# Gated delta branch: the log-decay sums as rows from two products, spread over the partitions through DRAM, and a pinned copy

## Chip, cores and metric

The kernel runs on one core of a Trainium2 chip. The metric is the device time of one execution in microseconds (us), lower is better. Five engines work side by side, each through its own instruction stream in order: TensorE (PE, with PEld for its weight loads), VectorE (DVE), ScalarE (ACT), GpSimd (POOL) and SyncE (SP), which here issues all transfers.

## What is computed

Two models of two layers each run one after the other on 256 tokens of width 1024: first feed-forward blocks, a hybrid mixer and a sparse attention, then a second model whose layers have three branches (a gated MLP, a retention, a gated delta rule) that are gated, projected and summed. The change touches only the gated delta branch, once in each of the two layers of the second model. Cut to what matters, for one direction:

```python
gc = jnp.cumsum(to_chunks(g[..., None], c)[..., 0], axis=-1)
decay = jnp.exp(jnp.where(incl, gc[..., :, None] - gc[..., None, :], -jnp.inf))
lower = jnp.where(strict, jnp.einsum("nbhid,nbhjd->nbhij", kb, kc) * decay, 0.0)
sol = lax.linalg.triangular_solve(lower + eye, rhs, left_side=True, lower=True)
```

`g` is the log decay of every token and head. The decay matrix needs its running sums once along the rows and once along the columns. There are 4 heads and two directions, forward and backward.

## The kernel before

**Staging.** Weights stream through SBUF in units of 1 MB (`raw`, three buffers, line 258). Each unit is turned in two halves into a high part (ACT, line 203) and a low part (DVE, line 207), with four buffers of halves, and each matrix product is three matmuls (lines 277 to 279). SP issues a load when the DVE part of the unit three before is done.

**Order.** A scheduler places the instructions of each engine by priority, which is program order, and by simulated times; an instruction that is ready earlier may float ahead. `keep_in_program_order` pins an instruction behind the instruction that was traced last on its engine.

**Two strands.** In `second` (line 191) a generator `delta` (line 206, the gated delta branch) is woven with a generator `others` (line 1491, gates, projections and the other branches). Each `yield n` in `delta` lets `others` trace n steps. The numbers stand in `SIDE` (line 1158). Steps 2 and 3 of `others` are a product of two weight units, 4 and 5 the next product, 6 and 7 the first half of a gate (`half(0, 0)`), 8 a small product of the MLP branch with the first unit of `half(0, 1)`.

**The stage of the change.** In `delta`, in order:

1. `narrow` and `softplus` give the log decays `gs` (lines 1212 to 1226), a tile of 128 tokens by 16 columns (direction, token half, head).
2. `keys(0, ...)` (line 1259) makes the keys `k` from two weight units. After each, one step of `others` is traced (2 and 3).
3. `yield SIDE[0]` traces steps 4 and 5 of `others`.
4. Four products (lines 1263 to 1266) give the running sums as columns, and line 1268 copies them to `gc`.
5. For each of four pairs of direction and token half, four products (line 1275) give the sum of one head each, repeated on all partitions: the column of `gs`, broadcast to 128 x 128, times a triangular mask. From that PSUM tile, DVE subtracts the column and caps into `D` (line 1279), ACT takes an Exp for the other chunk into `Dc` (line 1282, two of four pairs), and ACT an Exp over `D` (line 1283).
6. `scores` (line 1292) multiplies keys with keys (line 1297, PE) and with `D` and `Dc` (lines 1301 and 1305, DVE) into `U`.
7. POOL adds the two directions (line 1312), `yield SIDE[1]` traces steps 6 and 7, and `U[0]` goes to DRAM (line 1331) and comes back in blocks of 32 (line 1335). ACT turns one half of them (line 1337), and POOL solves the blocks in 31 steps (lines 1341 and 1343). ACT turns one half back (line 1344), SP sends the result to DRAM (lines 1350 and 1352) and fetches it again (line 1353) as `C`.
8. `yield SIDE[2]` traces step 8. Then come the queries (`keys(1, ...)`), their scores, the values (lines 1365 to 1370) and the copies of `C` (lines 1384 and 1386, ACT) that the rest of the solution is built on.

Of the kernel before, what the change touches and what calls it, by code (L numbers as in the profile page):

```python
# [12 lines left out]
AF = mybir.ActivationFunctionType  # L13
OP = mybir.AluOpType
AX = mybir.AxisListType
PSUM = bass.MemoryType.PSUM

D = 1024
T = 256
# [27 lines left out]
class Entry:  # L47
# [17 lines left out]
    def load(self, dram, between=None):  # L65
        self.raw.append(self.net.fetch(dram, 2048, between))
# [38 lines left out]
class Net:  # L105
# [43 lines left out]
    def dram(self, shape):  # L149
        self.n += 1  # L150
        return self.dp.tile(shape, F32, name=f"dram{self.n}")

    def load_const(self, name, cols, parts=128):
        t = self.const(cols, parts=parts)
# [348 lines left out]
    def start(self, dram):  # L503

        nc = self.nc
        self.x = [self.cp.tile([128, D], F32, name=f"x{t}") for t in range(2)]
        halves = lambda n: [slice(o, o + n // 2) for o in (0, n // 2)]
# [6 lines left out]
        with self.manual(mybir.EngineType.SP):  # L514
            a, b = halves(D)
            load(0, a)
# [337 lines left out]
def _parts(x, n, bits):  # L854

    out = []
    for _ in range(n):
# [9 lines left out]
         "Y00 C10 U11 C11 Q01 Y01 C12 | C13 M110 | M111 X10 |  | Y10 X11 |  | Q10 Q11 Y11 |  |  |  |  |  | "  # L867
         "W0 | D | W1 | D | ")
SHARE = ((0, 0), (0, 0), (1, 1), (1, 1), (1, 1), (1, 1))
# [285 lines left out]
            pass  # L1155


SIDE = (2, 2, 1, 1, 1, 1, 1, 1, 1, 2, 0)


class Second:
# [29 lines left out]
    def second(self, l, then, end=None):  # L1191
        nc, ins = self.nc, self.ins
        V, A, PE, G = nc.vector, nc.scalar, nc.tensor, nc.gpsimd
        mm = PE.matmul
# [4 lines left out]
        v4 = lambda a: a.rearrange("p (h c) -> p h c", h=4)  # L1199
# [6 lines left out]
        def delta(y_c):  # L1206

            yield SIDE[7]
            Y = [v24(self.g(1024)) for _ in range(2)]
# [14 lines left out]
            gs = self.small(16)  # L1224
# [13 lines left out]
            def keys(i, ss):  # L1238
# [3 lines left out]
                for gr in range(2):  # L1242
# [10 lines left out]
                    out.append(a)  # L1253
                    yield SIDE[8 + i]
                V.tensor_scalar(ss, pss[:, :8], EPS, None, op0=OP.add)
                return [out[h // 2][:, h % 2] for h in range(4)]

            ss, r, rq, nk = self.small(16), None, self.small(8), self.small(8)
            k = yield from keys(0, ss[:, :8])
            yield SIDE[0]  # L1260

            pc = self.pt()
            mm(pc[:, 0:8], self.tri, gs[:, 0:8], start=True, stop=True)
            mm(pc[:, 8:16], self.rtri, gs[:, 8:16], start=True, stop=True)
# [2 lines left out]
            gc = self.small(24)  # L1267
            V.tensor_copy(gc, pc[:, :24])
            D = [v24(self.g(1024)) for _ in range(2)]
            Dc = [v4(self.l2()) for _ in range(2)]  # L1270
            for d, t in order:
                pr = v4(self.pt())
                for h in range(4):
                    c = d * 8 + t * 4 + h
                    mm(pr[:, h, :], gs[:, c:c + 1].to_broadcast([128, 128]), self.rtri if d else self.tri,  # L1275
                       start=True, stop=True)
                for h in range(4):
                    c = d * 8 + t * 4 + h
                    V.scalar_tensor_tensor(D[d][:, t, h, :], pr[:, h, :], gc[:, c:c + 1], self.rcap if d else self.cap,
                                           op0=OP.subtract, op1=OP.min)  # L1280
                    if t != d:
                        A.activation(Dc[d][:, h, :], pr[:, h, :], AF.Exp, bias=gc[:, 16 + d * 4 + h:17 + d * 4 + h])
                A.activation(D[d][:, t], D[d][:, t], AF.Exp)

            rk = self.small(8)
# [26 lines left out]
            G.tensor_tensor(U[0], U[0], U[1], OP.add)  # L1312
            yield SIDE[1]

# [11 lines left out]
            B, turn = sq(flat(U[1])), sq(flat(X))  # L1326
            Z, back = sq(flat(Y[0])[:, :512]), flat(Y[0])[:, 512:].rearrange("p (i q) -> p i q", q=16)
            lower = slice(64, 128)
# [4 lines left out]
            for d in (1, 0):  # L1333
                for s in range(2):
                    nc.sync.dma_start((turn if d else B)[parts[d][s]],
                                      bass.AP(wide.tensor, wide.offset, [[129 * 32, 32], [128, 32], [1, 32]]))
            A.activation(B[lower].rearrange("p j i -> p i j"), turn[lower], AF.Copy)
            for e in range(31):
                n, m, cs = 31 - e, e // 2 + 1, slice(e + 1, 32)
                a = flat(Y[1])[:, :m * n].rearrange("p (q i) -> p q i", i=n)  # L1340
# [5 lines left out]
            for d in range(2):  # L1346
# [6 lines left out]
                nc.sync.dma_start(C[d].rearrange("p (m c) -> p m c", m=8), tight.rearrange("(m r) j c -> (r j) m c", r=4))  # L1353
            yield SIDE[2]
            q = yield from keys(1, ss[:, 8:])
            r = self.rsqrt(ss, 16, 1.0, 0.0)
# [7 lines left out]
            for gr in range(2):  # L1364
                ps = self.group_w(ww[4 + gr], hT)
                for j in range(2):
                    acc = conv(8 + 2 * gr + j, ps[j][:, :256])
                    for t in range(2):
                        c = (2 * gr + j) * 128
                        PE.transpose(pv[t][:, c:c + 128], acc[:, t * 128:(t + 1) * 128], self.ident)  # L1370
                yield SIDE[10]
            for t in range(2):
# [18 lines left out]
            for t in range(2):  # L1391
                for d in range(2):
                    c = C[2 * d].rearrange("p (t h c) -> p t h c", t=2, h=4)[:, t, :, None].to_broadcast([128, 4, 4, 32])
                    (G if d else V).tensor_tensor(r4(Y[d][:, t]), r4(bc4(self.near)), c, OP.mult)
            for lev in range(2):
                flip()
                T1 = []
                for t in range(2):
                    p = v4(self.pt())
# [5 lines left out]
                for t in range(2):  # L1405
                    p = v4(self.pt())
                    for h in range(4):
                        mm(p[:, h, :], T1[t][:, h, :], Y[1][:, t, h, :], start=True, stop=True)
                    a, b, keep = Y[0][:, t], Y[1][:, t], T1[t]
# [8 lines left out]
            for i in range(3):  # L1418
                for d in range(2):
                    a, b = (1, 0) if d else (0, 1)  # L1420
                    p = v4(self.pt())
                    for h in range(4):
                        if i == 1:
                            mm(p[:, h, :], Uc[d][:, h, :], W[d][:, a, h, :], start=True, stop=True)
                        else:
                            mm(p[:, h, :], Y[d][:, b if i else a, h, :], (r1[d] if i else vp[a])[:, h, :],
                               start=True, stop=True)
# [6 lines left out]
            for t in range(2):  # L1434
                po = v4(self.pt())
                d = 1 - t
# [13 lines left out]
                for h in range(4):  # L1450
                    V.scalar_tensor_tensor(v4(yo)[:, h, :], po[:, h, :], f[:, h:h + 1], v4(zd[t])[:, h, :],
                                           op0=OP.mult, op1=OP.mult)
# [161 lines left out]
        out = self.down_steps(ins["bout"][l], 8, mT.tok, self.add_x if then else self.finish(end), then)  # L1614
# [195 lines left out]
```

## Time and profile before

| | |
|---|---|
| median of 3 runs | 1719.06 us (1717.37 to 1719.6) |
| profiled execution, its own time | 1717.73 us |
| span of the profiled execution, first to last instruction | 1715.9 us |
| mean granted TensorE clock | 0.992 |
| busy PE / DVE / ACT / POOL | 98% / 66% / 52% / 17% of the span |
| DMA | 287.65 MB, mean 168 GB/s |
| longest chain, by engine | PE 82%, DVE 6%, POOL 5%, issue 3%, ACT 2%, DMA 2% |
| the two layers of the second model | from about 1095 to 1400 us and from 1400 us to the end |

The busy share of PE is an average and counts pipelined matmuls. What tells more is where PE sat idle, and which instruction it then waited for. Times below are positions in the span, in us from its first instruction; the second layer repeats the stage of the change some 308 us later.

### The profile page before, as it was taken

The page shows a single profiled execution, that of the slowest core. Times are in us where ns is not written, and L with a number is a line of the kernel's source. Part 1 is how long each engine was busy: PE and PEld are TensorE (multiplying, and loading weights), DVE is VectorE, ACT ScalarE, POOL GpSimd, SP SyncE. Part 2 cuts the span into 40 slices and gives each one's busy share as a digit, 9 for nine tenths or more (in the row PEclk, how much of TensorE's full clock was granted, in tenths as well). Part 3 has the DMA queues.
Part 4 walks back from the last instruction along what each step waited for, and adds up shares of the span by engine and source line. Part 5 has one row for each costly group of instructions (what it writes and reads, how often), then busy time and mean ns, then how long its engine had stood idle before and what let it go on. Part 6 is the DMA issues. An engine that isn't in the chain of part 4 may idle for free.

```text
span 1715.9 us, 27060 instructions
## 1 busy us (share of the span) xinstructions
PE 1686.2 (98%) x10518; PEld 1495.0 (87%) x10518; DVE 1130.9 (66%) x2203; ACT 896.4 (52%) x1329; POOL 299.4 (17%) x458
## 2 busy tenths in 40 slices
PE   9999999999999999999899999999999999999998
PEld 8998799788999899988689998888898878889886
DVE  7665588656665566647956664657775765778566
ACT  7443476464444354434465444567446446644643
POOL 3000021002000010000331000234532113364211
PEclk9999999999999999999899999999999999999999
DMA  7555453444555555554125556445443544554442
GB/s 274 197 176 205 150 193 127 147 152 159 194 193 188 176 193 191 182 205 161 68 99 180 189 189 212 167 153 168 142 151 143 184 165 175 149 163 158 146 148 96
DMA packets 63440, 287.65 MB, mean 168 GB/s; under 512 B 23760, under 2 KB 26704, under 8 KB 30288
## 3 DMA queue, kind: packets, MB, share of 16 engines
q1 hardware_dynamic: 63312, 285.92, 48.3%
q8 instruction: 83, 1.36, 0.3%
q14 instruction: 45, 0.37, 0.1%
HBM read 283.28 MB, written 2.62 MB: 167 GB/s over the span
## 4 chain that ended last, share of the span: by engine, by line
PE 82%; DVE 6%; POOL 5%; issue 3%; ACT 2%; DMA 2%; SPq 0%; POOLq 0%; ACTq 0%; DVEq 0%
PE mm L278 25%; PE mm L279 25%; PE mm L277 24%; DVE lo L207 2%; POOL g L1343 2%; POOL g L1341 2%; DMA g<-dram 1%; PE tr L435 1%; ACT hi L203 1%; DVE g L85 0%; DVE g L1010 0%; PE tr L1275 0%; PE tr L1583 0%; PE tr L687 0%; PE tr L1401 0%
## 5 line engine op out<-in xcount | busy, mean ns | idle before, releaser
L207 DVE TENSOR_TENSOR lo<-raw,hi 128x512 fp32r<-128x512 f32 (+1 forms) x1032 | 696.5, 718 | 433.4 <-ACT hi L203 432.2
L203 ACT ACTIVATE hi<-raw 128x1024 fp32r<-128x1024 f32 (+1 forms) x526 | 546.7, 1045 | 542.9 <-PE mm L279 239.6
L278 PE MATMUL mm<-g,hi 128*128 128x256 f32 x1760 | 496.7, 282 | 0.0
L277 PE MATMUL mm<-g,hi 128*128 128x256 f32 x1760 | 495.3, 282 | 0.8 <-ACT hi L203 0.8
L279 PE MATMUL mm<-g,lo 128*128 128x256 f32 x1760 | 495.8, 283 | 0.0
L277 PEld LDWEIGHTS mm<-g,hi 128*128 128x128 f32 x1760 | 333.2, 189 | 2.2 <-ACT hi L203 1.2
L278 PEld LDWEIGHTS mm<-g,hi 128*128 128x128 f32 x1760 | 333.1, 189 | 0.7
L279 PEld LDWEIGHTS mm<-g,lo 128*128 128x128 f32 x1760 | 332.4, 189 | 0.3 <-issue 0.2
L277 PE MATMUL mm<-hi,g 128*128 128x512 f32 (+1 forms) x784 | 313.2, 400 | 0.7 <-ACT g L203 0.7
L278 PE MATMUL mm<-lo,g 128*128 128x512 f32 (+1 forms) x784 | 311.5, 398 | 1.2 <-DVE lo L207 0.7
L279 PE MATMUL mm<-hi,g 128*128 128x512 f32 (+1 forms) x784 | 309.6, 396 | 1.0 <-DVE g L448 1.0
L279 PEld LDWEIGHTS mm<-hi,g 128*128 128x128 f32 x784 | 147.7, 189 | 35.9 <-DVE g L448 1.9
L278 PEld LDWEIGHTS mm<-lo,g 128*128 128x128 f32 x784 | 148.1, 189 | 35.1 <-DVE lo L207 5.0
L277 PEld LDWEIGHTS mm<-hi,g 128*128 128x128 f32 x784 | 148.0, 189 | 32.5 <-ACT g L203 1.2
L278 PE MATMUL mm<-lo,f 128*128 128x512 f32 x416 | 164.7, 396 | 0.2 <-POOL lo L207 0.2
L279 PE MATMUL mm<-hi,f 128*128 128x512 f32 x416 | 163.9, 396 | 0.0
L277 PE MATMUL mm<-hi,f 128*128 128x512 f32 x416 | 161.4, 398 | 0.0
L214 POOL TENSOR_SCALAR sm<-sm 128x1 f32<-128x1 f32 x18 | 7.8, 431 | 576.7 <-ACT c L70 576.0
L278 PEld LDWEIGHTS mm<-lo,f 128*128 128x128 f32 x416 | 78.1, 188 | 19.5 <-POOL lo L207 0.6
L279 PEld LDWEIGHTS mm<-hi,f 128*128 128x128 f32 x416 | 78.1, 188 | 18.6
L277 PEld LDWEIGHTS mm<-hi,f 128*128 128x128 f32 x416 | 78.1, 188 | 18.2
L90 POOL TENSOR_TENSOR g<-x,g 128x512 f32<-128x512 f32 x12 | 15.4, 1292 | 216.1 <-DVE x L499 170.2
(408 smaller groups left out, 1666.8 us busy)
## 6 DMA issues: line engine op xcount, KB each, us to landing
raw<-in_wgw_dram SPq DMA_DIRECT2D x80, 1024.0 KB, 4.9
raw<-in_wdn_dram SPq DMA_DIRECT2D x44, 1024.0 KB, 4.9
raw<-in_bx_dram SPq DMA_DIRECT2D x24, 1024.0 KB, 4.8
raw<-in_bgate_dram SPq DMA_DIRECT2D x24, 1024.0 KB, 4.8
raw<-in_bw_dram SPq DMA_DIRECT2D x20, 1024.0 KB, 4.8
raw<-in_hyx_dram SPq DMA_DIRECT2D x12, 1024.0 KB, 4.8
raw<-in_bproj_dram SPq DMA_DIRECT2D x12, 1024.0 KB, 4.9
raw<-in_hyw_dram SPq DMA_DIRECT2D x10, 1024.0 KB, 4.9
```

The lines of the kernel that those rows point to most:

```text
L90: self.nc.gpsimd.tensor_tensor(self.src[t][:, s], self.net.x[t][:, s], self.gain[:, s], OP.mult)
L203: nc.scalar.activation(hi, src, AF.Copy)
L207: (nc.gpsimd if o and help else nc.vector).tensor_tensor(lo[..., s], src[..., s], hi[..., s].bitcast(F32), OP.subtract)
L214: G.tensor_scalar(r, v, add, EPS, op0=OP.add, op1=OP.add)
L277: mm(out, a[0], b[0], start=start, stop=False)
L278: mm(out, a[0], b[1], start=False, stop=False)
L279: mm(out, a[1], b[0], start=False, stop=stop)
L435: self.nc.tensor.transpose(p[:, k, :], src[:, k * 128:(k + 1) * 128], self.ident)
L1341: G.tensor_tensor(a, Z[:, :m, e:e + 1].to_broadcast([128, m, n]), B[:, e:e + 1, cs].to_broadcast([128, m, n]), OP.mult)
L1343: G.tensor_tensor(Z[:, :m, cs], Z[:, :m, cs], a, OP.add)
```

## The change

The running sums of the 8 columns of one direction are made as 8 rows by one product (columns of `gs` as the stationary side, the triangular mask as the moving side), two products in all. ACT copies the two 8 x 128 results to SBUF, one transfer writes them to DRAM (8 KB), and two transfers read them back (8 rows of 128 for each direction), the same 4 KB to every partition, straight into `D` (512 KB each). The products are pinned behind the keys. `yield SIDE[0]` (steps 4 and 5) moves behind the two reads. The subtraction works in place in `D`, so the Exp for the other chunk is now traced ahead of it. Two instructions of that loop are pinned, the first subtraction and the first Exp for the other chunk of each such pair. Step 8 of `others` is traced ahead of the turning copy (line 1337) instead of behind the solution, and that copy is pinned.

```diff
+    def rows(self, products):
+        nc, n, b = self.nc, products[0][0].shape[-1], len(products)
+        p, r = self.pt(), self.t2()
+        for i, (cols, mask) in enumerate(products):
+            self.tc.keep_in_program_order(nc.tensor.matmul(p[:n, i * 128:(i + 1) * 128], cols, mask, start=True, stop=True))
+        nc.scalar.activation(r[:n, :b * 128], p[:n, :b * 128], AF.Copy)
+        d = self.dram([b, n, 128])
+        nc.sync.dma_start(d.rearrange("b n c -> n b c"), r[:n, :b * 128].rearrange("n (b c) -> n b c", b=b))
+        return d
+
+    def spread(self, out, d, first, n):
+        self.nc.sync.dma_start(out, bass.AP(d.tensor, d.offset + first * 128, [[0, 128], [1, n * 128]]))
...
-SIDE = (2, 2, 1, 1, 1, 1, 1, 1, 1, 2, 0)
+SIDE = (2, 2, 0, 1, 1, 1, 1, 1, 1, 2, 0)
...
             k = yield from keys(0, ss[:, :8])
-            yield SIDE[0]
-
+            gs_rows = self.rows([(gs[:, 0:8], self.tri), (gs[:, 8:16], self.rtri)])
             pc = self.pt()
...
             D = [v24(self.g(1024)) for _ in range(2)]
+            for d in range(2):
+                self.spread(D[d].rearrange("p t h c -> p (t h c)"), gs_rows, 8 * d, 8)
             Dc = [v4(self.l2()) for _ in range(2)]
+            yield SIDE[0]
             for d, t in order:
-                pr = v4(self.pt())
                 for h in range(4):
                     c = d * 8 + t * 4 + h
-                    mm(pr[:, h, :], gs[:, c:c + 1].to_broadcast([128, 128]), self.rtri if d else self.tri,
-                       start=True, stop=True)
-                for h in range(4):
-                    c = d * 8 + t * 4 + h
-                    V.scalar_tensor_tensor(D[d][:, t, h, :], pr[:, h, :], gc[:, c:c + 1], self.rcap if d else self.cap,
-                                           op0=OP.subtract, op1=OP.min)
                     if t != d:
-                        A.activation(Dc[d][:, h, :], pr[:, h, :], AF.Exp, bias=gc[:, 16 + d * 4 + h:17 + d * 4 + h])
+                        i = A.activation(Dc[d][:, h, :], D[d][:, t, h, :], AF.Exp, bias=gc[:, 16 + d * 4 + h:17 + d * 4 + h])
+                        if h == 0:
+                            self.tc.keep_in_program_order(i)
+                    i = V.scalar_tensor_tensor(D[d][:, t, h, :], D[d][:, t, h, :], gc[:, c:c + 1],
+                                               self.rcap if d else self.cap, op0=OP.subtract, op1=OP.min)
+                    if c == 0:
+                        self.tc.keep_in_program_order(i)
                 A.activation(D[d][:, t], D[d][:, t], AF.Exp)
...
-            A.activation(B[lower].rearrange("p j i -> p i j"), turn[lower], AF.Copy)
+            yield 1
+            self.tc.keep_in_program_order(A.activation(B[lower].rearrange("p j i -> p i j"), turn[lower], AF.Copy))
```

## Rows read from the trace of the kernel before

**Rows 1.** The page's first part: busy us, share of the span, instructions.

```profile
PE 1686.2 (98%) x10518; PEld 1495.0 (87%) x10518; DVE 1130.9 (66%) x2203; ACT 896.4 (52%) x1329; POOL 299.4 (17%) x458
```

**Rows 2.** Windows of 10 us: width, busy us (instructions) of PE, PEld, DVE, ACT, POOL, clock, DMA.

```profile
1150.00:1160.00 10.00, 10.00 (x61) 8.90 (x61) 7.84 (x25) 7.08 (x14) 3.40 (x4) 1.00 0.34 124
...
1220.00:1230.00 10.00, 7.62 (x40) 6.03 (x40) 5.38 (x11) 3.98 (x6) 0.00 (x0) 1.00 0.78 234
```

**Rows 3.** Waits of PE, 1070 us to the end: total us, times, longest.

```profile
PE tr L1370 <- DVE t L1235: 4.4, 4, 1.4
```

**Rows 4.** Timeline of ACT, first layer: start, us, instruction, idle before and its releaser.

```profile
1215.95 1.10 ACT L1344 ACTIVATE g<-g 64x512 f32<-64x512 f32 x1 [9.02 <-POOL g L1343]
...
1225.42 0.42 ACT L1386 ACTIVATE g<-g 128x256 f32<-128x256 f32 x1 [5.61 <-DMA g<-dram]
```

**Rows 5.** Timeline of SP: issues of weight loads on both sides of the transfers of the solution.

```profile
1203.39 0.33 SPq L258 DMA_DIRECT2D raw<-in_bx_dram  x1
...
1218.76 0.61 SPq L258 DMA_DIRECT2D raw<-in_bw_dram  x1
```

**Rows 6.** Timeline of POOL: the addition, the first and the last step of the solution.

```profile
1168.67 2.39 POOL L1312 TENSOR_TENSOR g<-g,g 128x1024 f32<-128x1024 f32 x1 [15.18 <-DVE g L1301]
...
1182.12 0.24 POOL L1341 TENSOR_TENSOR g<-g,g 128x31 f32<-128x31 f32 x1 [11.06 <-ACT g L1337]
...
1215.68 0.23 POOL L1343 TENSOR_TENSOR g<-g,g 128x16 f32<-128x16 f32 x1
```

**Rows 7.** Timeline of PE: the products of the sums (a product is two instructions).

```profile
1136.98 0.28 PE L1263 MATMUL tr<-sm,c 128*128 128x8 f32 x2
...
1149.81 3.82 PE L1275 MATMUL tr<-c,sm 128*128 128x128 f32 x32
1153.38 0.48 PE L277 MATMUL mm<-hi,g 128*128 128x512 f32 x1
```

**Rows 8.** DVE: a window over the decay stage (columns of Rows 2), then its timeline.

```profile
1150.98:1168.78 17.80, 17.80 (x95) 15.26 (x94) 15.78 (x48) 12.03 (x22) 2.53 (x4) 1.00 0.34 119
...
1139.81 1.29 DVE L207 TENSOR_TENSOR lo<-raw,hi 128x512 fp32r<-128x512 f32 x2 [3.02 <-ACT hi L203]
...
1150.98 1.12 DVE L1279 SCALAR_TENSOR_TENSOR g<-tr,sm,c 128x128 f32<-128x128 f32 x4 [0.70 <-PE tr L1275]
...
1168.44 0.34 DVE L1305 SCALAR_TENSOR_TENSOR l<-l,sm,tr 128x128 f32<-128x128 f32 x1
```

**Rows 9.** Groups by line and shape: total us, mean ns | idle before, releaser.

```profile
L196 ACT ACTIVATE t<-tr 16x256 f32<-16x256 f32 x2 | 0.7, 352 | 0.0
...
L1282 ACT ACTIVATE l<-tr,sm 128x128 f32<-128x128 f32 x16 | 5.2, 361 | 3.0 <-DVE g L1279 3.0
...
L1279 DVE SCALAR_TENSOR_TENSOR g<-tr,sm,c 128x128 f32<-128x128 f32 x32 | 9.3, 342 | 2.6 <-PE tr L1275 1.4 <-ACT l L1282 1.2
...
L85 DVE SCALAR_TENSOR_TENSOR g<-x,sm,g 128x512 f32<-128x512 f32 x8 | 5.6, 748 | 3.8 <-POOL sm L217 3.8
```

**Rows 10.** DMA issues by tensor: count, KB each, median us from issue to landing.

```profile
raw<-in_bgate_dram SPq DMA_DIRECT2D x24, 1024.0 KB, 4.8
...
g<-dram SPq DMA_DIRECT2D x12, 128.0 KB, 4.9
...
f<-in_gln_dram SPq DMA_DIRECT2D x2, 512.0 KB, 3.7
...
dram<-g SPq DMA_DIRECT2D x8, 64.0 KB, 2.4
```

**Rows 11.** Timeline of SP and ACT where the new transfers and the copies would stand.

```profile
1137.74 1.09 ACT L1511 ACTIVATE f<-mm 128x512 f32<-128x512 f32 x2
...
1141.16 0.33 SPq L258 DMA_DIRECT2D raw<-in_bgate_dram  x1
...
1161.03 1.06 ACT L203 ACTIVATE hi<-raw 128x1024 fp32r<-128x1024 f32 x1
...
1179.92 2.12 ACT L1337 ACTIVATE g<-g 64x1024 f32<-64x1024 f32 x1 [0.48 <-DMA g<-dram]
```

## The prediction, made before the changed kernel ran

> **What bounds the kernel now.** I read the page first. PE is busy in 98% of the span and no other engine is near that [rows 1], so an edit pays if it takes work from PE or closes one of its few gaps. Busy shares by window come next. Where the sums are made PE has no gap (10.00 of 10 us), but behind the block solution it has one (7.62 of 10 us) [rows 2]. The waits name it: the transposes of line 1370 waited 4.4 us in four waits, 2.2 us a layer [rows 3].
>
> That gap is the end of a chain, read backwards. ACT stood 9.02 us until POOL had finished its 31 steps, then 5.61 us until the solution was back from DRAM at 1225.42 [rows 4]. SP issues in order too: between its weight loads of 1203.39 and 1218.76 stand the writes that wait for POOL [rows 5]. So ACT and SP stand still, the stock of converted weights runs out, and PE stops. POOL starts its 31 steps at 1182.12, after the addition of 1168.67 and the way through DRAM, and ends them at 1215.91 [rows 6]. The addition waits for the last score on DVE, at 1168.44 to 1168.78, and the DVE stage that ends there starts at 1150.98 [rows 8]. **At this one place the start of the decay stage sets the end, and not PE's work alone.** Elsewhere it is PE's work.
>
> **Part 1, PE.** Removed: 16 products a layer, 32 instructions, from 1149.81 to the start of the next at 1153.38, 3.57 us or 0.112 us each [rows 7]. Added: two products, which move the same 128 columns, four instructions, 0.45 us (bounds: 0.28 us for two instructions with few columns, so 0.56 us, and nothing) [rows 7]. Net 3.1 us a layer. They lie on PE's own path.
>
> **Part 2, when the decays start.** The two row products are pinned behind the keys' last traced step, where the first product of the column sums already stood, at 1136.98 [rows 7]. The steps to the landing:
> - ACT's copy of 8 x 256 is near the copy of 16 x 256, 0.35 us [rows 9]. It stands behind the two copies that end at 1138.83 [rows 11], so it is done at about 1139.2.
> - The write of 8 KB I price as the 64 KB writes, 2.4 us (below 2.4 it may be; above, the 512 KB load, 3.7) [rows 10]: 1141.6. SP's issue waits for it. A weight load of 1141.16 [rows 11] may be caught behind the wait for under 1 us; its second half is converted at 1161.03 [rows 11], and a load lands in 4.8 us [rows 10], so some 14 us hide it.
> - The two reads of 512 KB have no like: no transfer in this trace reads one row for all partitions. The nearest are 3.7 us for 512 KB alone and 4.9 for the small reads from DRAM, some of which queue behind a weight load [rows 10]. With that load in front I take 5.5 for the first, which lands at 1147.1, and 1.1 more for the second (4.8 less 3.7, the price of 512 KB more [rows 10]), at 1148.2. Below: 3.7 from 1141.6, at 1145.3. Above: each read takes a whole load's 4.8 and both stand behind one load, 1151.2 and 1156.0.
>
> DVE is no bar: the first subtraction is pinned behind the last conversion of step 5, and counting conversions back from PE's order that is the pair at 1139.81 [rows 8]. So the stage starts at 1147.1 instead of 1150.98, 3.9 us earlier.
>
> **Part 3, the length of the stage.** It lasts 17.80 us, 15.78 of them busy on DVE [rows 8]. A subtraction costs 342 ns from PSUM. From SBUF it is worth the same: 748 ns for 512 columns [rows 9] leaves 342 at 128, if each column costs 1.06 ns. An Exp costs 361 ns [rows 9] at most from either. That the Exp now goes ahead of the subtraction in place is no new kind of wait: today the two waited for each other as well, 3.0 and 1.2 us over both layers [rows 9]. The scores need not wait for PSUM tiles that the sums held. Of the 2.02 us in which DVE stood I take half away, 1.0 (bounds: nothing, and 2.0). Together the chain to the addition ends 4.9 us earlier.
>
> **Part 4, step 8 and the turning copy.** The same steps of the other strand are traced in total, so no work is added. The pin puts the copy behind step 8's second conversion, which ran at 1161.03, long before the copy at 1179.92 [rows 11]; 4.9 us earlier it is still behind. Nothing, with 14 us of cover; if that cover were gone, 1.06 us for one conversion [rows 11].
>
> **Sum.** At the gap PE arrives 3.1 us earlier, and the solution 4.9. PE's gap of 2.2 shrinks to 0.4, so the layer ends 4.9 us earlier; the most is 3.1 + 2.2 = 5.3. Two layers: 9.8 us, at most 10.6. The profiled execution took 1717.73 us by itself, 1.3 under the median; its span of 1715.9 would be 1706.1. I put the sum on the median: 1719.06 - 9.8 = **1709.3 us**.
>
> **A rule that would change the sum.** No row shows the rate of 128 partitions that read the same 4 KB; a plain load of 1 MB takes 4.8 us [rows 10]. The Trainium skill, in DMA: Bandwidth & Descriptors, section Latency and other measured facts, reports that rows which fall on the same HBM channels are read at about half rate (207 against 103 GB/s), and calls the mechanism an inference. No run here shows it yet.
>
> **Rivals.**
> 1. *The reads at half rate.* Each 512 KB costs 1.1 us more [rows 10], so the second lands 2.2 us later and the chain is 2.7 us earlier. Two layers give 5.4: 1713.7. For it: all rows are one address. Against: 4 KB reads are as long as those of a load. The rule above is this case.
> 2. *PE's saving alone.* The gap of line 1370 is gone or stays for its own reasons, because the engines' orders are made anew. Gain 2 x 3.1 = 6.2: 1712.9. For it: PE waited there for DVE, not by name for the solution [rows 3]. Against: the two waits of ACT just ahead [rows 4].
> 3. *The change does not do what it says.* The copy, the write or the conversions are placed so that the decays start no earlier. Then PE arrives 3.1 us earlier at a solution that comes when it did, and the gap grows from 2.2 to 5.3. Gain nothing: 1719. For it: the wait for POOL and the one for DRAM bind ACT today [rows 4], so less PE work alone is worth nothing there. Against: gaps on ACT and DVE around 1139 to 1150 leave room [rows 8, 11].
> 4. *Slower: the reads land late.* DVE stands at the pinned subtraction while the conversions of the next weights queue behind it. With 1.0 from part 3 the gain is gone when the stage starts at 1152.0, and 0.2% is lost from 1153.7. By the upper bound of part 2 the second read lands at 1156.0; the second of the four pairs needs it, about 1.1 us into the stage (four subtractions, 1.12 [rows 8]), so that the stage counts as starting at 1154.9. Then 2.9 us a layer are lost, 5.8 in all: 1724.9. For it: two transfers and a wait in a row in place of a product that needed none, in a queue that also carries the weights. Against: every row of a like size lands in under 5 us [rows 10].
>
> **How the numbers follow.** A measurement of this kernel tells about 0.2%, 3.4 us, from no change. The forecast has 0.50, rival 1 0.10, rival 2 0.07, rival 3 0.18, rival 4 0.15. Faster: 0.50 + 0.10 + 0.07 = 0.67; same 0.18; slower 0.15. The forecast's own range is 1706.5 (the most, 10.6, less the 2 us by which runs differ) to 1713. The range reaches up through rivals 1 to 3 and over the milder part of rival 4, to 1721, and leaves out the rest of it, about one in ten, and some of the low end.
>
> **What would show it.** No products at line 1275 and two new ones at about 1137. The first subtraction before 1149, the addition on POOL near 1164, the first of the 31 steps near 1177, the last near 1211. ACT's wait at line 1386 no longer than today's, and the waits of line 1370 near 0.8 in total. Part 2 is wrong if the reads land more than 10 us after the write; part 3, if the window from the first subtraction to the last score is over 18 us; the chain as such, if POOL starts earlier and PE still ends where it did. The whole prediction is wrong if PE has a new gap of several us between 1137 and 1180.

## The result, and the profile after

The changed kernel is slower by 0.6%: median 1729.37 us (20 runs, 1726.73 to 1736.79) against 1718.20 us for the kernel before on the same chips (20 runs, 1715.74 to 1740.3). The ratio is 1.0059, 95% interval 1.004 to 1.0078. The forecast was 1709.3 us, with 1721 as the upper end. The profiled execution after took 1729.21 us, span 1727.4, 11.5 more than the span before.

Line numbers after are 15 to 18 higher. The page's first part first:

```profile
PE 1685.4 (98%) x10462; PEld 1491.0 (86%) x10462; DVE 1129.3 (65%) x2203; ACT 898.1 (52%) x1333; POOL 302.9 (18%) x458
```

There are 56 matmul instructions fewer than in [rows 1], 28 a layer as predicted, and yet the span is longer. The timeline of PE in the first layer (start, us, instruction, idle time before it and its releaser) shows the parts of the change in place, and where the time went:

```profile
1135.77 0.60 PE L158 MATMUL tr<-c,sm 128*8 128x128 f32 x4
...
1148.62 0.39 PE L292 MATMUL mm<-hi,g 128*128 128x512 f32 x1
1148.84 0.39 PE L293 MATMUL mm<-lo,g 128*128 128x512 f32 x1
...
1226.06 0.66 PE L1388 MATMUL tr<-c,t 128*128 128x128 f32 x2 [5.94 <-DVE t L1250]
...
1227.80 0.63 PE L292 MATMUL mm<-hi,g 128*128 128x512 f32 x1
1228.23 0.63 PE L293 MATMUL mm<-lo,g 128*128 128x512 f32 x1
```

The four instructions of the row products stand at 1135.77. At 1226.06 PE comes out of a gap of 5.94 us, before the same transposes that waited 2.2 us a layer in [rows 3]. Behind it a product of 512 columns follows the last one after 0.43 us; at 1148 it was 0.22. The waits of PE from 1070 us to the end (total us, times, longest) hold both layers:

```profile
PE tr L1388 <- DVE t L1250: 11.5, 2, 5.9
PE mm L292 <- DVE t L1250: 4.1, 4, 1.4
```

The first row was 4.4 before; the second is new. Windows of 10 us (the columns of [rows 2]; the last three numbers are granted clock, DMA share, GB/s):

```profile
1150.00:1160.00 10.00, 10.00 (x46) 8.30 (x45) 8.06 (x23) 8.78 (x15) 2.55 (x2) 1.00 0.51 183
1180.00:1190.00 10.00, 7.47 (x50) 6.29 (x49) 5.96 (x10) 9.15 (x14) 8.08 (x19) 1.00 0.48 175
...
1220.00:1230.00 10.00, 4.06 (x13) 3.19 (x12) 7.72 (x15) 5.65 (x9) 0.00 (x0) 0.76 0.73 228
1230.00:1240.00 10.00, 10.00 (x44) 8.05 (x43) 3.70 (x7) 4.27 (x5) 2.04 (x2) 0.90 0.41 136
...
1540.00:1550.00 10.00, 9.67 (x34) 7.77 (x35) 6.02 (x12) 2.39 (x4) 0.00 (x0) 0.70 0.60 211
```

In 1220 to 1230 PE is busy for 4.06 us (7.62 in [rows 2]) and the clock is 0.76: part of the window ran at 1.2 instead of 2.4 GHz, which is what the doubled spacing of the products shows. In the second layer the same comes at 1540.

**The balance.** The idle gaps of PE in the second model (from 1070 us on) sum to 22.2 us after and 10.2 before, so +12.0: the transposes 11.5 against 4.4, and 4.9 in new gaps around 1184 to 1188 and in layer two. The clock missing in the windows under full clock (10 us times one minus the clock, without the last window) is 10.2 us after and 5.1 before, so about +5.1. Behind the two long gaps alone it is 6.8; a stretch of low clock at 1120 to 1140, ahead of the change, was 1.7 us shorter in this execution. The removed products give back about 5.8 (measured below). 12.0 + 5.1 - 5.8 = 11.3, of 11.5. The clock term is rough; in the experiments the same balance is off by 1 to 3 us.

**Why PE starves at 1220.** The timeline of ACT before, between the two waits of [rows 4]:

```profile
1217.07 1.06 ACT L203 ACTIVATE hi<-raw 128x1024 fp32r<-128x1024 f32 x1
1218.04 0.46 ACT L1233 ACTIVATE t<-mm,c 128x256 f32<-128x256 f32 x1
1218.40 1.05 ACT L203 ACTIVATE hi<-raw 128x1024 fp32r<-128x1024 f32 x1
1219.34 0.47 ACT L1233 ACTIVATE t<-mm,c 128x256 f32<-128x256 f32 x1
```

And after:

```profile
1178.33 2.11 ACT L1355 ACTIVATE g<-g 64x1024 f32<-64x1024 f32 x1 [5.79 <-DMA g<-dram]
...
1215.20 1.11 ACT L1362 ACTIVATE g<-g 64x512 f32<-64x512 f32 x1 [9.20 <-POOL g L1361]
1220.85 0.42 ACT L1404 ACTIVATE g<-g 128x256 f32<-128x256 f32 x1 [4.54 <-DMA g<-dram]
1221.17 1.04 ACT L218 ACTIVATE hi<-raw 128x1024 fp32r<-128x1024 f32 x1
...
1226.03 0.47 ACT L1248 ACTIVATE t<-mm,c 128x256 f32<-128x256 f32 x1
```

Before, two weight conversions and two convolution steps stood between the copy back (1344) and the copy C[3] (1386), and ACT did them while the solution was in flight. After, C[3] (1404) stands right behind the copy back (1362). ACT has nothing else in order, so the pairs of conversion and convolution start only at 1221.17, one behind another. The first transposes need the first of these convolution steps (ACT, 1222.12), which DVE finishes behind its own parts of the conversions; in this row the first of the two instructions ends at 1225.91, and PE goes on at 1226.06:

```profile
1225.44 0.86 DVE L1250 SCALAR_TENSOR_TENSOR t<-mm,c,t 128x255 f32<-128x255 f32 x2
```

The wait for DRAM itself is shorter than before (4.54 against 5.61), and the copy runs 4.57 us earlier. **What changed is what stands behind it.** SP's timeline says why the copy itself could come earlier:

```profile
1138.74 0.34 SPq L161 DMA_DIRECT2D dram<-t  x1
...
1140.27 0.85 SPq L166 DMA_DIRECT2D g<-dram  x2
...
1215.20 1.34 SPq L1370 DMA_DIRECT2D dram<-g  x2
...
1218.21 2.09 SPq L1371 DMA_DIRECT2D g<-dram  x2
1220.39 9.63 SPq L273 DMA_DIRECT2D raw<-in_bw_dram  x3
```

No weight load stands between the solution's writes and its reads, as one did in [rows 5]. The first two rows are the new write and the two spreading reads. The turning copy (1355) too has moved one conversion forward; it waits 5.79 us where it waited 0.48 [rows 11], and the gaps at 1184 to 1188 follow.

### The profile page after: what moved, and what is told of

The parts are those of the page before. It is cut to its first block, busy times and chain, and to the rows that moved or that the text cites. A ratio compares the mean times of both kernels' runs of the same rounds, so it can differ in the third digit from the quotient of the medians.

```text
span 1727.4 us, 26974 instructions
## 1 busy us (share of the span) xinstructions
PE 1685.4 (98%) x10462; PEld 1491.0 (86%) x10462; DVE 1129.3 (65%) x2203; ACT 898.1 (52%) x1333; POOL 302.9 (18%) x458
## 4 chain that ended last, share of the span: by engine, by line
PE 81%; DVE 6%; POOL 5%; ACT 3%; issue 3%; DMA 2%; SPq 0%; POOLq 0%; ACTq 0%; DVEq 0%
PE mm L293 25%; PE mm L294 25%; PE mm L292 24%; DVE lo L222 2%; POOL g L1361 2%; POOL g L1359 2%; DMA g<-dram 1%; PE tr L450 1%; ACT hi L218 1%; DVE g L85 0%; DVE g L1025 0%; DMA dram<-g 0%; PE tr L702 0%; PE tr L1601 0%; PE tr L1419 0%
```

## The experiments

"Idle" is the sum of PE's gaps in the second model. In every run the kernel before was timed on the same chip. The names in brackets are those that the expectations use.

| run | median us (runs) | ratio to before, 95% interval | span | idle |
|---|---|---|---|---|
| change without its turning part (e1) | 1731.36 (10) | 1.0055 (1.0024 to 1.0086) | 1729.6 | 22.9 |
| change, C[3] held late (e3) | 1718.18 (12) | 0.9983 (0.9962 to 1.0004) | 1714.5 | 13.6 |
| before, C[3] held late (e4) | 1716.91 (12) | 0.9987 (0.9958 to 1.0015) | 1714.5 | 8.7 |
| before, C[3] early (e5) | 1730.84 (10) | 1.006 (1.0031 to 1.009) | 1728.2 | 16.7 |
| change, C[3] late, turning copy on POOL (e9) | 1716.81 (12) | 0.9994 (0.9978 to 1.0009) | 1712.2 | 12.6 |
| the same, addition on DVE (e7) | 1718.24 (10) | 0.9987 (0.9962 to 1.0012) | 1713.2 | 13.1 |
| the same, copy back on POOL (e10) | 1718.91 (12) | 0.9997 (0.9982 to 1.0013) | 1717.5 | 13.2 |
| before, with all four edits (e11) | 1716.04 (12) | 0.9991 (0.9958 to 1.0025) | 1715.4 | 8.0 |
| change, all four, short solution (e12) | 1706.57 (10) | 0.9919 (0.9891 to 0.9947) | 1704.2 | 6.7 |
| before, all four, short solution (e13) | 1714.32 (10) | 0.997 (0.9938 to 1.0001) | 1710.0 | 6.7 |
| change, C[3] late, both copies on POOL (e14) | 1718.94 (12) | 0.9997 (0.9965 to 1.0029) | 1717.6 | 13.6 |
| the same, transfers behind the solution on POOL's queue (e16) | 1709.96 (4) | 0.9954 (0.9937 to 0.997) | 1709.2 | 7.6 |
| the same, two of the four reads on POOL's queue too (e17) | 1709.30 (4) | 0.9954 (0.9939 to 0.9969) | 1707.5 | 8.2 |
| before, C[3] late, both copies and these transfers on POOL (e18) | 1716.39 (10) | 0.999 (0.9974 to 1.0006) | 1713.9 | 8.9 |

### Which part of the change makes the loss

The turning part alone undone:

```diff
-            yield 1
-            self.tc.keep_in_program_order(A.activation(B[lower]..., turn[lower], AF.Copy))
+            A.activation(B[lower]..., turn[lower], AF.Copy)
```

(and the step count of step 8 back to 1.)

> The rows and their spread stay; the turning copy is placed as in the kernel before (no pin, step 8 behind the solution). Theory A (the loss is ScalarE standing at two copies whose data is still in flight, at places in its stream that the rows and the spread have brought about): same as the changed kernel, 1727 to 1732 us, turning copy still waiting 5 to 6 us a layer. Rival B (the pin of the turning copy, and step 8 ahead of it, cost the time): back to 1718 us or below.

The loss stays whole, with gaps of 6.01 and 6.11 us at the same transposes, and the turning copy still waits 5.68 us. The turning part is not the cause; the loss came with the rest: the rows, their transfers, the moved steps 4 and 5 and the pins of the decay loop. These were not taken apart.

Next the copy C[3] held at its traced place in the changed kernel, and the same edit in the kernel before:

```diff
-            A.activation(C[3], C[0], AF.Copy)
+            late(A.activation(C[3], C[0], AF.Copy))
```

> The changed kernel with the copy of the solution (C[3] from C[0]) pinned behind the other late copy, so that ScalarE converts weights in place of waiting for that transfer. Theory A: the waits of PE at the transposes of the values (11.5 us in two) fall below 2 us in all, the stretches at the low clock behind them go too (some 5 us), the 4.9 us of gaps behind the turning copy stay: 1712 to 1716 us. Rival C (the loss is the new transfers, which keep weight loads back, on SyncE's queue or in bandwidth): nothing changes, 1727 to 1732 us.

> The kernel before with the same pin. Theory A: its own gap at the transposes of the values, 4.4 us in both layers, closes: 1713 to 1716 us. Rival D (that gap is set by the end of the solution itself, as I had forecast, and not by where ScalarE waits for it): no change, 1717 to 1720 us.

One copy of 0.42 us a layer, held back, takes 11 to 13 us from the changed kernel (11.2 between the medians, 12.9 between the spans), with all its new transfers in place. The median lies 2 us above the range that was expected. Waits of PE in that run:

```profile
PE mm L292 <- DVE t L1250: 3.8, 4, 1.5
PE tr L1388 <- DVE t L1250: 2.3, 2, 1.1
```

The 11.5 of line 1388 is 2.3; the gaps behind the turning copy are still there, at full clock. In the kernel before the pin is worth nothing that can be told in the time. Of its waits at the transposes, however, less than half is left:

```profile
PE tr L1370 <- DVE t L1235: 1.9, 2, 1.0
```

There were two such waits a layer (0.94 us at 1221.99 and 1.43 at 1229.17 in the first), and the pin took away the second, which stood behind the copy.

Now the reverse, in the kernel before, with none of the new products or transfers: C[3] is traced ahead of the product of zd, whose weights' conversions then come behind it on ACT (the later line of the copy goes).

```diff
-            for p in self.group_x(wx[0:2], hT):
-                zd.append(self.l2())
-                A.activation(zd[-1], p, AF.Silu)
+            with self.tc.issue_after(A.activation(C[3], C[0], AF.Copy).ins):
+                for p in self.group_x(wx[0:2], hT):
+                    zd.append(self.l2())
+                    A.activation(zd[-1], p, AF.Silu)
```

> The kernel before, no new transfer, but with the copy of the solution traced ahead of the product of the gate's weights and those weights' conversions issued behind it on ScalarE, as they stand in the changed kernel. Theory A: PE's gap grows from 2.2 to some 7 to 9 us a layer, with a stretch at the low clock behind it: 1731 to 1740 us. Rival C: no change, 1717 to 1720 us.

It loses as much as the change (1.006), a little less than was expected. Timeline of ACT in that run:

```profile
1217.21 0.84 ACT L1233 ACTIVATE t<-mm,c 128x256 f32<-128x256 f32 x2
1225.56 0.42 ACT L1377 ACTIVATE g<-g 128x256 f32<-128x256 f32 x1 [7.51 <-DMA g<-dram]
1225.88 2.93 ACT L203 ACTIVATE hi<-raw 128x1024 fp32r<-128x1024 f32 x3
```

PE's timeline, and the window around it:

```profile
1226.97 0.79 PE L277 MATMUL mm<-hi,g 128*128 128x512 f32 x1 [5.47 <-ACT hi L203]
```

```profile
1220.00:1230.00 10.00, 4.53 (x20) 3.40 (x19) 3.05 (x6) 4.44 (x6) 0.00 (x0) 0.82 0.49 132
```

The three conversions wait behind the copy, PE waits 5.47 us for them, and the clock falls. Idle rose by 6.5 us and the span by 12.3; the windows at 1220, 1230 and 1540 miss 1.8 + 1.6 + 3.4 = 6.8 us of clock. So an early place of this copy in ACT's order is enough for a loss of this size, and holding it late takes the loss away. Both directions are shown, with one difference: here three conversions for zd stand behind the copy, in the change the pairs of conversion and convolution. What made the new order was not tried.

### Why the saved work still did not come through

With C[3] late the changed kernel is level with the one before, where PE's saving should make it some 6 us faster. C[3] stays late, and three more edits come one on another: the turning copy on POOL, then the addition on DVE, then the copy back on POOL. The control has all four in the kernel before.

```diff
-            self.tc.keep_in_program_order(A.activation(B[lower]..., turn[lower], AF.Copy))
+            G.tensor_copy(B[lower]..., turn[lower])
...
-            G.tensor_tensor(U[0], U[0], U[1], OP.add)
+            V.tensor_tensor(U[0], U[0], U[1], OP.add)
...
-            A.activation(back[lower]..., Z[lower], AF.Copy)
+            G.tensor_copy(back[lower]..., Z[lower])
```

> The changed kernel with the copy of the solution pinned late as in e3, and the turning copy on GpSimd, which has nothing else to do there and needs its result. Theory A: the gaps of PE behind the turning copy (4.7 us in e3) go, those at the transposes (2.3 us) stay: 1712 to 1715 us. Rival C (transfers hold the weights back): as e3, 1717 to 1719 us. Rival E (the copy is slower on GpSimd, so the solution ends later and that sets the end): 1718 us or more.

> As e9, with the addition of the two directions on VectorE in place of GpSimd, where it took 4.8 us instead of 2.4 because conversions ran beside it. The solution should end 3 to 4 us earlier. If the end of the solution sets PE's last gap there (ScalarE waits for GpSimd at the copy back), the 2.3 us of gaps at the transposes go: 1710 to 1713 us. If it does not: as e9.

> As e7, with the copy back from the solution on GpSimd too, so that ScalarE waits for no transfer and for no GpSimd step in this stage. Theory A: no gap of PE between 1140 and 1240 us, and so the saving of PE's work (6.2 us) and the old gap (4.4 us) both come through: 1708 to 1712 us.

> The kernel before with the same three moves (solution copy pinned late, turning copy and copy back on GpSimd, addition on VectorE), without rows and spread. Theory A: no gap of PE in the stage, and the products of the sums still on PE, so 6.2 us more than e10: 1714 to 1717 us. If rows and spread cost something of their own that the gaps have hidden: less than 4 us between e10 and this.

No ratio can be told from 1. The first and the third miss their ranges; the second came out by its other branch, as the first; the control lies in its range, but the freed change was to be 6.2 us faster than it and is not. The gaps moved each time. With the turning copy on POOL, its gaps went and the transposes waited more:

```profile
PE tr L1388 <- DVE t L1250: 5.9, 2, 3.3
```

With ACT free of all three copies, the wait stands one stage on, at the transposes of the near level, which need the solution itself:

```profile
PE tr L1336 <- DVE g L1412: 6.5, 4, 2.5
```

The addition on DVE bought nothing. In the run with all three copies off ACT its result was written at 1167.57; with the addition and only the turning copy on POOL that was at 1169.91. But the earlier write stood behind a weight load of 1166.47 and landed in 6.4 us, the later one in 3.5. DMA issues in the run with all three copies off ACT, 1160 to 1190:

```profile
dram<-g SPq DMA_DIRECT2D x1, 512.0 KB, 6.4
```

This looked like a solution that is late against PE. To test that, its steps 16 to 30 were cut to the first of their blocks, in both freed kernels; the rest of those steps is left out, so the time is that of less work on POOL. The orders on PE, DVE and ACT are unchanged.

```diff
-                n, m, cs = 31 - e, e // 2 + 1, slice(e + 1, 32)
+                n, m, cs = 31 - e, e // 2 + 1 if e < 16 else 1, slice(e + 1, 32)
```

> This is the changed kernel freed at every point (C3 copy held behind, turning copy and copy back on GpSimd, addition on VectorE), with the products and additions of the solution's steps 16 to 30 cut to the first of their blocks, so the result of those steps is left out; TensorE, VectorE and ScalarE keep their order. The freed kernel's span was 1717.5 us with 13.2 us of TensorE idle in the second model, of which 2.48 + 0.91 and 2.23 + 0.88 stand before the products of the near level (waiting for the solution). Theory (the chain from the decays through the solution bounds the stage, because its start moved by about 1 us only where TensorE's work shrank by 3.1 a layer): the steps end 5 to 7 us earlier, those four gaps go, idle falls to about 6.7, the granted clock returns to 1 in the windows around 1230 to 1250 and 1540 to 1560, and the span comes to 1706 to 1711 (-6.5 of gaps, -2 to -3 of clock, the rest as before); against the kernel before a ratio of 0.993 to 0.996. Rival (TensorE is held by something else there, ScalarE's or VectorE's own work or the weight loads): the gaps turn up again within 10 us at another wait, idle stays above 10, span 1714 to 1718.

> The same cut of steps 16 to 30 in the kernel before with the same four freedoms, which had a span of 1715.4 us and 8.0 us of idle, of it 0.79 and 0.58 before the products of the near level. Theory: only those 1.4 us go; span 1713 to 1715.5, ratio 0.997 to 1.000. The difference to the short form of the changed kernel is then the whole of the TensorE work that the change removes, 5 to 7 us. Rival: the short form gains as much here as in the changed kernel (more than 5 us), because the solution bounds both alike, or neither gains.

As the theory said, the gaps at 1336 are gone in both and idle is 6.7 us in both; both spans lie 2 to 3 us below the ranges that were expected. They differ by 1710.0 - 1704.2 = **5.8 us. That is PE's saving**, 2.9 us a layer. (The medians differ by 7.7; the control's profiled execution is one of its fastest.) It had been there all along, hidden in waits behind the solution. The cut also let SyncE issue its weight loads in another order, so one thing was open: the late solution, or the loads behind it. In the freed change with the addition on POOL, ACT and SP show this:

> Complete computation: the changed kernel with the C3 copy held behind, turning copy and copy back on GpSimd, and the addition left on GpSimd as in the change (VectorE's addition made the write stand behind a weight load: it landed in 6.4 us against 3.5). Theory: the solution starts 0.6 us earlier than with VectorE's addition and the gaps before the near level's products are 2 to 3 us a layer instead of 3.1 to 3.4, with no wait at the transposes of the values; idle 11 to 12.5, span 1711 to 1715, ratio 0.996 to 0.9995. Rival (the wait of ScalarE at the copy back was not the cost): as the kernel with the copy back on ScalarE, 0.9994, within 1 us.

```profile
1231.85 1.06 ACT L218 ACTIVATE hi<-raw 128x1024 fp32r<-128x1024 f32 x1 [6.31 <-DMA raw<-in_bw_dram]
```

```profile
1219.22 2.92 SPq L1368 DMA_DIRECT2D dram<-g  x1
1225.83 0.38 SPq L1371 DMA_DIRECT2D g<-dram  x1
1226.32 1.46 SPq L273 DMA_DIRECT2D raw<-in_bw_dram  x3
```

That run by itself was another miss (0.9997, idle 13.6). But three weight loads stand on SP behind the read of 1225.83, which waits for the write of 1219.22, and ACT stands 6.31 us until one of them lands. The next copies of the solution stand behind that conversion. The last three runs move only queues:

```diff
-                        nc.sync.dma_start(tight..., back[parts[d][s]])
+                        nc.gpsimd.dma_start(tight..., back[parts[d][s]])
...
-                        nc.sync.dma_start(tight..., Z[parts[d][s]])
-                nc.sync.dma_start(C[d]..., tight...)
+                        nc.gpsimd.dma_start(tight..., Z[parts[d][s]])
+                nc.gpsimd.dma_start(C[d]..., tight...)
```

> Complete computation: the freed changed kernel with the addition on GpSimd (span 1717.6 us, idle 13.65, of it 2.95 + 0.30 and 2.79 + 0.89 before the near level's products), with one more edit: the transfers behind the solution (its result to DRAM and back, eight issues a layer) go from SyncE's queue to GpSimd's. There ScalarE stood 6.31 us at a conversion whose weight load SyncE issued only at 1226.32, behind the solution's last read, which waited for its write. Theory (the solution holds TensorE through SyncE's queue: weight loads stand behind its transfers): the weight loads come 5 us or more earlier, ScalarE's wait goes, the four gaps shrink to under 1 us together, idle 6.7 to 8, clock 1 again around 1230 to 1240 and 1540 to 1560, span 1705 to 1711, ratio 0.992 to 0.996. Rival (the solution's end itself is too late, whatever queue carries it): the gaps stay at 2 to 4 us a layer, span 1714 to 1718.

> The kernel before with the same freedoms (C3 copy held behind, turning copy and copy back on GpSimd, transfers behind the solution on GpSimd's queue). Theory: its gaps there were 0.8 and 0.6 us, so at most 1.5 to 3 us are to be had: span 1711 to 1715, ratio 0.996 to 1.000; the changed kernel in the same form is then 5 to 7 us faster, the TensorE work that the change removes. Rival: the queue was the bound in both, and this form gains as much as the changed kernel's, the two within 2 us.

The changed kernel so edited is faster than both kernels, 0.9954 (0.9937 to 0.997), with nothing left out; the control stays at 0.999. The medians differ by 6.4 us, the spans by 4.7, and the four runs of the one lie below all ten of the other. SP and ACT in the fast one:

```profile
1209.51 19.23 SPq L273 DMA_DIRECT2D raw<-in_bw_dram  x4
```

```profile
1234.04 0.44 ACT L1402 ACTIVATE g<-g 128x256 f32<-128x256 f32 x1 [1.76 <-DMA g<-dram]
```

SP issues its four loads from 1209.51 with no transfer of the solution between them. ACT's 6.31 us wait is gone, and the gaps at 1336 are 0.9 us in all instead of 6.9. The solution itself is no earlier: from the issue of its first write to the end of its last step it takes 46.8 us in this run (1172.12 to 1218.96) and in the one before (1168.12 to 1214.97). PE, DVE and ACT have the same order of instructions in both. So it was the queue that held PE, not the solution's end. Whether the two copies must be on POOL as well was not tried.

Last, two of the four reads into the solution on POOL's queue too, so that their 3.7 us of issuing run side by side:

```diff
-                    nc.sync.dma_start((turn if d else B)[parts[d][s]],
+                    (nc.gpsimd if s else nc.sync).dma_start((turn if d else B)[parts[d][s]],
```

> The kernel of the run before with two of the four reads into the solution issued by GpSimd too, so that the four issues (3.7 us one behind another on SyncE) run side by side. Theory: the solution starts 1 to 2 us earlier, but nothing waits for it any more: within 1 us of the run before. Rival (the solution's end is the bound): 2 to 4 us faster than the run before, at gaps that shrink by 1 to 2 us a layer.

No difference that can be told: 1709.30 against 1709.96. From the end of the addition to the first step it takes 11.7 us in both.

## Why the prediction was wrong

**Part 1, PE: right.** 3.1 us a layer predicted, 2.9 by the spans of the two short runs.

**Part 2, the start: right, in part by luck.** DVE's timeline, and the window from the first subtraction to the last score:

```profile
1146.89 1.14 DVE L1296 SCALAR_TENSOR_TENSOR g<-g,sm,c 128x128 f32<-128x128 f32 x4 [1.15 <-DMA g<-dram]
...
1164.69 2.49 DVE L222 TENSOR_TENSOR lo<-raw,hi 128x512 fp32r<-128x512 f32 x4
...
1168.13 2.47 DVE L222 TENSOR_TENSOR lo<-raw,hi 128x512 fp32r<-128x512 f32 x2
```

```profile
1146.89:1164.77 17.88, 17.88 (x85) 14.87 (x83) 15.94 (x48) 16.14 (x24) 2.67 (x3) 1.00 0.36 126
```

The first subtraction came at 1146.89; 1147.1 was forecast. The two reads issued at 1140.27 land like loads that queue behind a load (DMA issues, 1130 to 1180):

```profile
g<-dram SPq DMA_DIRECT2D x2, 512.0 KB, 6.9
```

The first landed 6.5 us after its issue, where 5.5 had been taken; but the write of 8 KB, which the reads wait for, took 1.5 us at most (1138.74 to 1140.27) and not 2.4, and the two errors cancel. That a 512 KB transfer lands in 6.9 us is no exception: the trace before has such loads at 5.7 to 6.4 beside those of [rows 10], so "every row of a like size lands in under 5 us" holds for the rows shown alone. DVE was nearer to being a bar than was read: its last conversion before the first subtraction ran until 1145.74. The second read landed about 1.3 us behind the first, near the 1.1 of a plain 512 KB and not the 2.2 of rival 1, and no pair of subtractions waited for it, so rivals 1 and 4 fall. The half rate that the Trainium skill reports, in DMA: Bandwidth & Descriptors, section Latency and other measured facts, was measured on copies with row pitches of 4 and 8 MiB; for 128 partitions that read one 4 KB row these rows do not show it.

**Part 3, the length: wrong in size.** The stage lasted 17.88 us, not 16.8: nothing of the 2.02 us came back, the lower bound. (The price of a subtraction from SBUF held, 1.14 us for four against 1.12, but its working did not show it: the 1.06 ns a column are the difference of the two rows that it compares.) The scores still ended about 4 us earlier than in [rows 8]. Then the addition, which the prediction moved along at its old 2.39 us, took 4.80. POOL's timeline:

```profile
1164.65 4.80 POOL L1329 TENSOR_TENSOR g<-g,g 128x1024 f32<-128x1024 f32 x1 [9.49 <-DVE g L1318]
...
1180.51 0.24 POOL L1359 TENSOR_TENSOR g<-g,g 128x31 f32<-128x31 f32 x1 [11.06 <-ACT g L1355]
...
1214.94 0.23 POOL L1361 TENSOR_TENSOR g<-g,g 128x16 f32<-128x16 f32 x1
```

It is 4.8 us in both layers, as in every run of the changed kernel with POOL's addition. DVE's conversions start at 1164.69, within 0.04 us of the addition. In the kernel before DVE reached the next pair only at 1170.20, 1.5 us into the addition of 1168.67, and there the pair took longer, not the addition:

```profile
1170.20 2.01 DVE L207 TENSOR_TENSOR lo<-raw,hi 128x512 fp32r<-128x512 f32 x2
```

The four at 1164.69 run at their usual 0.62 us. If the addition stood still for these 2.49 us and then took its 2.39, that makes 4.9, and the pair at 1168.13 (2.47 us against 1.29 in [rows 8]) would wait for its end at 1169.45. In the same way the pair of before would wait 0.86 us for the addition's end at 1171.06 and take 2.1. The Trainium skill, in SBUF — State Buffer, section Who interferes with whom, says that a VectorE instruction with two SBUF inputs contends with a GpSimd one that reads SBUF, and calls the port pair that they share an exclusive lock; these rows agree, but no run here took the conversions away. So the steps began 1.6 us earlier (1180.51), not 4.9, and ended 0.7 earlier than in [rows 6].

**Part 4 and the sum: the step that failed.** The prediction moved the stage and left the orders of ACT and SP as they stood: the turning copy "nothing, with 14 us of cover", and at the gap only two arrival times, PE 3.1 earlier and the solution 4.9. But the change made the orders anew. The turning copy lost one conversion of its cover and C[3] lost two conversions and two convolution steps. That cost 12.0 us of idle and about 5 us of clock. The forecast that the solution comes 4.9 us earlier nearly came true at the copy C[3], which ran 4.57 us earlier, but by luck: the steps ended only 0.7 us earlier, and the rest comes from the weight load that no longer stands ahead of the reads (they landed in a median of 5.5 us before and 2.3 after). With PE's work 2.9 us less a layer and the solution 4.57 us earlier the kernel still got slower, so it is the way from these two times to the end of the layer that failed, and not their sizes. Rival 2 named the new orders, and took them for harmless. Rival 3 had the right kind of end: PE's saving lost in the same waits. It gave no loss, because it kept the order. The slower rival had another mechanism, which did not occur.

**The clock was no term of the sum.** A gap of 5.94 us carried 2.4 + 1.0 us of missing clock behind it (0.76 and 0.90 in the two windows). Gaps of 0.94 and 1.43 us before, and of 1.40 us after at 1184, carried none (the windows 1180 and 1220 at 1.00). But the length of a gap does not tell it alone. In the kernel before, 1.52 us of idle at 1433, ahead of transposes with few columns, was followed by a low clock; with C[3] late and the turning copy on POOL a gap of 3.30 us at 1220.64 was not, and one of 2.60 at 1525.34 was. The window of before first, then two of that run:

```profile
1430.00:1440.00 10.00, 8.07 (x51) 7.59 (x50) 4.91 (x10) 5.82 (x8) 7.35 (x22) 0.83 0.48 177
...
1220.00:1230.00 10.00, 9.36 (x45) 7.67 (x46) 7.63 (x15) 4.29 (x6) 0.43 (x1) 1.00 0.96 314
...
1520.00:1530.00 10.00, 7.41 (x40) 6.26 (x39) 8.22 (x16) 5.76 (x9) 3.04 (x3) 0.83 0.89 213
```

**The signs.** Those of the start came true (first subtraction before 1149, addition near 1164). Those of the solution did not: the first step came at 1180.51 and not near 1177, the last at 1214.94 and not near 1211, and the waits of line 1370 are 11.5 us instead of 0.8. The sign against the chain as such fired: POOL starts earlier and PE does not end earlier. The sign against the whole, a new gap between 1137 and 1180, did not fire, because the new gaps stand at 1184 and 1220. "ACT's wait at line 1386 no longer than today's" was of no use: it is shorter, 4.54 us, and the loss is there.

## What to carry to other kernels

An edit that moves a stage in an engine's stream also moves its neighbours: before summing, list for every in-order stream (ACT and the DMA queue included) what stands behind each instruction that waits for a transfer, and price the case that this cover is gone. A long wait may cost nothing while useful work stands ahead of it, and a shorter one at a worse place may cost the whole gain. When a saving does not appear, look on the next engine for the wait that took it; here it went from ACT's order to the transposes that need the solution, where SP's queue held it, and with both freed (C[3] held late, the two copies and the solution's transfers on POOL) 0.9954 came out.

## What was not expected of the hardware

- The clock: in 1220 to 1230, behind a PE gap of 5.94 us, the granted clock was 0.76 and products of 512 columns came every 0.43 us instead of 0.22. The length of the gap alone does not tell it: in one run 3.30 us left the clock at 1.00 and 2.60 did not, and in the kernel before it fell behind 1.52.
- POOL's addition of 128x1024 took 4.80 us where four of DVE's conversions started with it, and a pair of conversions behind them 2.47 instead of 1.29. In the kernel before, where a pair started 1.5 us into the addition, the addition took 2.39 and the pair 2.01.
- The same 512 KB write landed in 3.5 us, or in 6.4 us behind a weight load issued 1.1 us before it (addition on DVE).
- Transfers issued from POOL's queue landed about as fast as from SP's, the four writes of 64 KB in a median of 4.3 us against 4.2 in the run before it. In both, in the first layer, two of the four landed in 2.2 to 2.7 us and the two amid a weight load in 5.9 to 6.5, so POOL's queue took them out of SP's order and not out of the loads' way. In the kernel before all four take 2.2 to 2.8. They cost POOL 0.9 to 1.6 us an issue or pair, at a time when it had little else in order.
